# Down products of 768 tokens by a recursion of seven, with the sums of their weights made earlier in the program

## The chip, the core and the metric

One core of a Trainium2 chip runs the whole program in one launch. The engines of a core work side by side, each in the order of its own instruction list, and wait for each other by semaphores: TensorE (PE, matrix products; PEld is its loading of weights), VectorE (DVE), ScalarE (ACT), GpSimd (POOL) and SyncE (SP). SP and POOL issue the transfers between memory and the core's own buffers. The metric is the device time of one execution in microseconds (us); shown are the median, the lowest and the highest of three runs.

## The reference

One layer of a decoder for 1024 prompt tokens and 8 sample tokens that share the weights (model width 1024, width of the feed-forward part 2816):

```python
z = x @ w_in                                   # all branches and gates
a = rg_lru(conv4(...)) * gelu(...)             # recurrent branch
s = window attention, 16 query heads, 4 kv heads, window 128
c = attention over 256 memory tokens, 4 heads
merged = sum(gate[n] * (branch[n] @ w_branch[n]))
h = layer_norm(ALPHA * x + merged @ w_out)
gt, up = split(h @ w_gate_up)
h = layer_norm(ALPHA * h + (silu(gt) * up) @ w_down)
```

Besides h it returns the states of the branches; among them are the window caches of the 8 sample rows, moved on by one token (`o_swk`, `o_swv`). Everything is in fp32.

## The kernel before, in words

Activations lie transposed: 128 channels on the partitions, tokens along the free axis, 1032 of them. An fp32 product is made of three passes of a reduced type (fp32r): every operand is split into a high part, cast by ACT, and a low part, subtracted by DVE (`split`, L79 to L83), and PE runs high by high, low row by high weight, high row by low weight, into one accumulator. So 128 by 128 weights against n tokens are three matmuls of n columns. Weights arrive in pieces of up to 128 by 512 (`half_raw`, 6 buffers, issued by SP) and are split into pairs (`half_pair`, 5 buffers of high and 4 of low parts).

The program has these stages, in order: the projection, whose products run by a recursion of seven (2 by 2 blocks, seven products for eight); the branches a and c with the attentions; branch s (from about 1035 us); the output projection with its layer norm; two feed-forward units made directly (f = 0, 1); twenty units by the recursion of seven (f = 2 to 21, up to 1668.9 us); the down products (to 1925.3 us); and the end of the last layer norm.

A unit f makes one block of 128 of the 2816 feed-forward channels for all tokens. `unit_step` (L1198) issues the seven products i = 0 to 6 of a unit, each for two parts p of 258 columns. The end of a unit on DVE and ACT (L1236 to L1241) makes the gated value `ft`, which SP stores to a scratch row `scr_f` in memory. `fast_quarter` makes the sums of weights that i = 1, 2, 4 and 5 take, and splits them three steps ahead.

The down products (`down`, L1296) have 8 output blocks m, 22 rows f and three chunks of tokens (384, 384 and 264 wide). For each chunk and output the weights are read again and split again (`streamed`, L1274); a row of a chunk is read from `scr_f` by POOL (L1292) and split into a pair `gh`, `gl` (`rows`, L1287). Rows of the next chunk are fetched three with each output. The first chunk opens four accumulators on rows 0 to 11 at once, since the last units' rows come last. Result and residual are put together by DVE (L1339), a running sum is kept for the layer norm (L1341, L1343), and the norm of a chunk (`layer_norm`, L992) is dealt out in steps between the outputs of the next chunk (`norm_step`). The last chunk has its own norm (`last_layer_norm`, L1030), which follows the products closely.

What sets the order: a scheduler puts each engine's instructions in order from the program and from buffers; rooms (`gd`) of freed stages are laid over each other, so a load can start when the last reader of the stage that had the room is through. `issue_after(x)` holds instructions of x's own engine behind x.

Of the kernel before, what the change touches and what calls it, by code (L numbers as in the profile page):

```python
# [10 lines left out]
F32 = mybir.dt.float32  # L11
# [13 lines left out]
CH = ((0, 384), (384, 384), (768, 264))  # L25
# [4 lines left out]
DIRECT_AT = ((0, 258), (258, 258), (516, 252), (768, 264))  # L30
ROOMS = (*range(83, 67, -1), *range(36, 4, -1), *range(67, 36, -1), *range(4, -1, -1))
EARLY, EARLY_ROWS = ("mm", "s", "mm", "s"), 12
NORM_AT = (0, 1, 3, 4)
LATE = 4
# [24 lines left out]
class Builder:  # L59
# [223 lines left out]
    def fast_quarter(self, st, i):  # L283

        nc, ((a11, a12), (a21, a22)), u = self.nc, st["raw"], st["u"]
        if i in (1, 2, 4, 5):
            src = self.w1.tile([P, D // 2], F32, tag="sum", name=f"us{u}_{i}", bufs=self.sums)
# [693 lines left out]
    def col_mean(self, s, n, name):  # L981

        nc = self.nc
        hi = self.ph.tile([P, 384], F32R, tag="lh", name=f"{name}h", bufs=1)[:, :n]
        lo = self.ph.tile([P, 384], F32R, tag="ll", name=f"{name}l", bufs=1)[:, :n]
        self.split(hi, lo, s)
        ps = self.bank("o", f"{name}p")[:, :n]
# [4 lines left out]
    def layer_norm(self, c, r, s1, gcol, emit, name, late=False):  # L992
# [5 lines left out]
        mu = self.col_mean(s1, n, f"{name}mu{c}")  # L998
        s2 = ph.tile([P, 384], F32, tag="s2", name=f"{name}s2{c}", bufs=1)[:, :n]
        for m in range(KT):  # L1000
            nc.vector.tensor_sub(r[m], r[m], mu)
            sq = s2 if m == 0 else ph.tile([P, 384], F32, tag="sq", name=f"{name}sq{c}_{m}", bufs=2)[:, :n]
# [5 lines left out]
        var = self.col_mean(s2, n, f"{name}va{c}")  # L1008
        rs = ph.tile([P, 384], F32, tag="s2", name=f"{name}rs{c}", bufs=1)[:, :n]
# [20 lines left out]
    def last_layer_norm(self, n, r, product, gcol, emit):  # L1030
# [4 lines left out]
        tile_ = lambda tag, name, bufs, dt=F32: ph.tile([P, 384], dt, tag=tag, name=name, bufs=bufs)[:, :n]  # L1035
        s1, s2 = tile_("s1", "ls1", 1), tile_("s2", "ls2", 1)
        hi, lo = (ph.tile([P, n], F32R, tag=f"c0{e}", name=f"c0{e}", bufs=1) for e in "hl")
        e1, e2 = self.bank("t", "le1")[:, :n], self.bank("t", "le2")[:, :n]
# [13 lines left out]
        for m in range(KT):  # L1052
            ps = product(m, last=m < LATE)
            if m in NORM_AT:
                self.norm_step()
# [4 lines left out]
            if m == 1:  # L1060
                s = tile_("xres", "lc0", 3)
                nc.vector.tensor_add(s, r[0], r[1])
                self.split(hi, lo, s)
            elif m == LATE - 1:
                with self.tc.issue_after(self.last_mm):
                    c0 = self.bank("o", "c0")[:, :n]
# [11 lines left out]
        mu, rs = tile_("xres", "lmu", 3), tile_("gt", "lrs", 3)  # L1078
# [14 lines left out]
    def out_proj(self, merged):  # L1093
# [4 lines left out]
        for c, (t0, n) in enumerate(CH):  # L1098
            s1 = ph.tile([P, 384], F32, tag="s1", name=f"o1s{c}", bufs=1)[:, :n]
            rs = []  # L1100
            for m in range(KT):
                if c == 0:
                    w[m] = self.resident(io["wout"][m], KT, f"wo{m}", 0)
                ps = self.mm_res(w[m], merged, c, f"op{m}_{c}", tag=("mm", "s")[m % 2])
                if m in NORM_AT:
                    self.norm_step()
                xr = ph.tile([P, 384], F32, tag="xres", name=f"xres{m}_{c}", bufs=2)[:, :n]
# [17 lines left out]
    def direct_units(self):  # L1125
# [31 lines left out]
        for n, m, q in ((0, 0, 0), (3, 4, 0), (5, 4, 2)):  # L1157
            self.ht[n] = [[self.hl(m + k, (q + p) * QN, QN) for p in range(2)] for k in range(4)]
# [5 lines left out]
    def h_sums(self, i):  # L1164
# [12 lines left out]
        x = lambda kh, th, k: self.accs[4 * kh + k][:, th * HT:(th + 1) * HT]  # L1177
# [3 lines left out]
        for k in range(4):  # L1181
            if i == 1:
                t1 = wide("t1", k)
                nc.vector.tensor_sub(t1, x(0, 0, k), x(0, 1, k))
                pair(1, k, t1)
            elif i == 2:
                t3, t2 = wide("t3", k), wide("t2", k)
                nc.vector.tensor_sub(t3, x(1, 1, k), x(0, 1, k))
                nc.vector.tensor_add(t2, t3, x(0, 0, k))
# [3 lines left out]
            else:  # L1193
                t4 = wide("t4", k)
                nc.vector.tensor_sub(t4, self.t2[k], x(1, 0, k))
                pair(6, k, t4)

    def unit_step(self, st, i):  # L1198
# [3 lines left out]
        for p in range(2):  # L1202
# [32 lines left out]
            elif i == 5:  # L1235
                nc.vector.tensor_add(za[:, hi_], d, st["s", 2, p])  # L1236
# [345 lines left out]
```

## Time and profile before

| | |
|---|---|
| median of three runs (lowest to highest) | 1938.64 us (1937.28 to 1940.72) |
| the profiled execution, and its span | 1940.76 us, 1939.0 us |
| mean granted TensorE clock | 0.996 |
| PE busy | 1906.2 us (98%), 14356 matmuls |
| DVE busy | 1361.8 us (70%) |
| ACT busy | 1017.7 us (52%) |
| POOL busy | 154.0 us (8%) |
| the down stage's matmuls (L1283, L1284, L1285) | 528 each |
| read from memory, written | 214.64 MB, 66.85 MB |

The profile's rows name line, engine, operation and tiles (out<-in) and then the shape. Matmuls are pipelined: a row's duration overlaps the next one's, and what a matmul takes of PE's time is the distance from start to start. `dl` is an accumulator of the down stage, `wd_h` and `wd_l` are parts of a piece of its weights, `gh` and `gl` parts of a row, `fb` and `fd` accumulators of a unit, `bsH` and `bsL` the rows of branch s, `n2s` the running sum of squares in the second layer norm.

### The profile page before, as it was taken

Reading aid. Unit: us, or ns where it says so; the run is one execution under the profiler, and the core shown is the slowest. Engines: PE = TensorE matmul, PEld = TensorE weight load, DVE = VectorE, ACT = ScalarE, POOL = GpSimd, SP = SyncE. Lnnn points to the kernel's source line nnn. Section 1 sums busy time; section 2 is a strip of 40 time slices with the busy share of each in tenths; the row PEclk is TensorE's granted clock in tenths of the full one; section 3 lists DMA queues with packets and bytes.
Section 4 is the critical chain, followed back from the end, with each engine's and each line's share of the span. In section 5 each row is a group of like instructions: output and inputs, shape, how many; then the busy total and the mean of one; then the engine's idle time right before and its main releaser. Section 6 shows DMA issues by size and latency. Waiting matters only on the chain. (4 is left out here: it accounts for less than half of the span.)

```text
span 1939.0 us, 37975 instructions
## 1 busy us (share of the span) xinstructions
PE 1906.2 (98%) x14356; PEld 1882.2 (97%) x14356; DVE 1361.8 (70%) x2875; ACT 1017.7 (52%) x2198; POOL 154.0 (8%) x242
## 2 busy tenths in 40 slices
PE   8999999999999999999999999999999999999997
PEld 8999999999999999999999999999999999999997
DVE  8678887887777545379887558965665666747566
ACT  5465565456566545388875245643333433635444
POOL 1000000000011310022110000000000000402001
PEclk9999999999999999999999999999999999999999
DMA  7444545465323876567625241122222322846554
GB/s 232 145 161 147 170 169 186 131 204 181 126 91 127 285 239 202 158 177 201 173 77 183 88 150 42 39 88 88 88 82 82 99 74 80 278 131 187 159 155 139
DMA packets 169383, 281.92 MB, mean 145 GB/s; under 512 B 20864, under 2 KB 83408, under 8 KB 169168
## 3 DMA queue, kind: packets, MB, share of 16 engines
q1 hardware_dynamic: 163280, 262.62, 43.1%
q0 software_dynamic: 5920, 16.88, 2.6%
q8 instruction: 112, 1.84, 0.4%
q14 instruction: 71, 0.58, 0.1%
HBM read 214.64 MB, written 66.85 MB: 145 GB/s over the span
## 5 line engine op out<-in xcount | busy, mean ns | idle before, releaser
L1285 PE MATMUL dl<-gh,wd_l 128*128 128x384 f32 (+1 forms) x528 | 168.1, 318 | 3.1 <-DVE wd_l L82 3.1
L1283 PE MATMUL dl<-gh,wd_h 128*128 128x384 f32 (+1 forms) x528 | 167.7, 318 | 1.1 <-ACT gh L81 1.1
L1284 PE MATMUL dl<-gl,wd_h 128*128 128x384 f32 (+1 forms) x528 | 167.9, 318 | 0.0
L1285 PEld LDWEIGHTS dl<-gh,wd_l 128*128 128x128 f32 x528 | 99.7, 189 | 3.5 <-DVE wd_l L82 3.5
L1283 PEld LDWEIGHTS dl<-gh,wd_h 128*128 128x128 f32 x528 | 99.7, 189 | 1.3 <-ACT gh L81 1.3
L1284 PEld LDWEIGHTS dl<-gl,wd_h 128*128 128x128 f32 x528 | 99.8, 189 | 0.5 <-DVE gl L82 0.5
L1292 POOL DMA_DIRECT2D gl<-scr_f x66 | 35.6, 539 | 788.3 <-PE fb L1219 632.0
L81 ACT CAST u_1h<-us 128x512 fp32r<-128x512 f32 x48 | 29.8, 621 | 87.5 <-issue 43.5
L608 ACT ACTIVATE bp<-bp,bst 128x257 f32<-128x257 f32 (+1 forms) x128 | 62.3, 489 | 19.9 <-DVE bst L604 19.9
L81 ACT CAST u_2h<-us 128x512 fp32r<-128x512 f32 x48 | 29.7, 619 | 76.6 <-PE fb L1218 38.2
L289 DVE TENSOR_TENSOR us<-ur,ur 128x512 f32<-128x512 f32 x96 | 66.1, 688 | 4.3 <-DMA ur<-win 2.2
L289 DVE TENSOR_TENSOR us<-us,ur 128x512 f32<-128x512 f32 x96 | 66.2, 690 | 2.3
L82 DVE TENSOR_TENSOR u_6l<-ur,u_6h 128x512 fp32r<-128x512 f32 x48 | 33.9, 706 | 44.9 <-PE fb L1219 28.5
L117 PE MATMUL brs<-bsH,wbs_h 128*128 128x384 f32 (+1 forms) x192 | 61.0, 319 | 1.0 <-ACT bsH L81 1.0
L118 PE MATMUL brs<-bsL,wbs_h 128*128 128x384 f32 (+1 forms) x192 | 60.9, 318 | 0.3 <-DVE bsL L82 0.3
L119 PE MATMUL brs<-bsH,wbs_l 128*128 128x384 f32 (+1 forms) x192 | 60.9, 317 | 0.0
L82 DVE TENSOR_TENSOR u_4l<-us,u_4h 128x512 fp32r<-128x512 f32 x48 | 33.0, 688 | 39.7 <-PE fb L1219 27.4
L604 DVE CUSTOM_DVE_ANT_0 bp<-bs,mask,nsnk 128x256 f32<-128x256 f32 (+1 forms) x128 | 53.5, 459 | 5.2 <-PE bs L601 4.6
L82 DVE TENSOR_TENSOR u_5l<-us,u_5h 128x512 fp32r<-128x512 f32 x48 | 33.1, 690 | 30.0 <-PE fd L1219 14.5
L1237 ACT ACTIVATE ft<-za 128x516 f32<-128x516 f32 x40 | 25.5, 636 | 52.4 <-DVE za L1236 52.0
L81 ACT CAST u_5h<-us 128x512 fp32r<-128x512 f32 x48 | 29.9, 624 | 38.1 <-DVE us L289 24.9
L81 ACT CAST u_0h<-ur 128x512 fp32r<-128x512 f32 x48 | 29.8, 621 | 37.8 <-PE ub L306 20.1
(2022 smaller groups left out, 8123.4 us busy)
## 6 DMA issues: line engine op xcount, KB each, us to landing
ur<-win SPq DMA_DIRECT2D x112, 256.0 KB
ur<-wgu SPq DMA_DIRECT2D x80, 256.0 KB
scr_f<-ft SPq DMA_DIRECT2D x40, 258.0 KB
gl<-scr_f POOLq DMA_DIRECT2D x44, 192.0 KB, 4.1
dck<-cmk SPq DMA_DIRECT2D x32, 256.0 KB
dcv<-cmvT SPq DMA_DIRECT2D x32, 256.0 KB
st<-scr_q SPq DMA_DIRECT2D x32, 256.0 KB
scr_g<-za SPq DMA_DIRECT2D x10, 516.0 KB
```

The source lines that it names most:

```text
L81: ins = self.nc.scalar.copy(hi, src).ins
L82: self.nc.vector.tensor_sub(lo, src, hi.bitcast(F32))
L117: nc.tensor.matmul(ps, sh, mh, start=i == 0, stop=False)
L118: nc.tensor.matmul(ps, sh, ml, start=False, stop=False)
L119: self.last_mm = nc.tensor.matmul(ps, sl, mh, start=False, stop=closes and i == last).ins
L289: nc.vector.tensor_add(src, a, b)
L604: nc.vector.tensor_tensor_reduce(pg[g], s[:, u * 256:u * 256 + n], msk, 1.0, snk[:, g:g + 1], ALU.add, ALU.min, st[:, g:g + 1])
L608: nc.scalar.activation(x, x, AF.Exp, bias=st[:, g:g + 1], scale=-1.0, accum_out=st[:, 4 + g:5 + g])
L1283: nc.tensor.matmul(ps, sh, mh, start=k == 0, stop=False)
L1284: nc.tensor.matmul(ps, sh, ml, start=False, stop=False)
L1285: self.last_mm = nc.tensor.matmul(ps, sl, mh, start=False, stop=closes and k == NF - 1).ins
L1292: self.nc.gpsimd.dma_start(lo.bitcast(F32), self.scf[f][:, t0:t0 + n])
```

## The change

The 1032 tokens are seen as two halves of 516. Tokens 0 to 383 and 516 to 899 are the two sides of the recursion; the other 132 of each half are the rest (264). The 22 rows are two halves of 11, the 8 outputs are 4 pairs.

- The products of the 768 tokens: instead of 8 by 22 by 2 triples of matmuls, seven products (in the order 0, 3, 2, 1, 5, 4, 6), each 4 output pairs by 11 rows, 384 wide. Each of them takes either stored rows and stored weights or sums of such. A column (one pair's output) is 33 matmuls, with its weights in three pieces (4, 4 and 3 rows).
- The rest: 8 outputs by 22 rows by three matmuls of 264, in two halves of 11 rows; the first halves of m = 0 to 3 run ahead. The low parts of the weights of products 0, 3 and 6 are kept in rooms and used again here; for these pieces only the cast is made again.
- The sums of weights for products 1, 2, 4, 5: 16 jobs (`sum_turn`, `sum_load`, `sum_weights`), each 4 loads by POOL, 4 additions by DVE and 4 stores by POOL to a scratch. Eight are dealt out between the products of branch s, eight between the steps of the units f = 2 to 10.
- The sums of rows for products 1, 2, 4 and 6 (`row_load`, `row_sums`): ten jobs in the units f = 11 to 20, each 2 loads by POOL, 4 operations of DVE and 4 stores (from POOL, the last of these from SP). The eleventh (`last_sums`) runs after product 0 by SP.
- Rows: each product reads its 11 rows by POOL, in the course of the product before it.
- The end of the last unit (f = 21, i = 5 and 6: `unit_end`) is held back and issued behind the split of the first eight rows.
- The parts p of a unit are now the two halves of 516 tokens, and a store of `ft` is one contiguous piece for each. The chunks of the earlier stages are 384, 390 and 258 wide.
- The window caches are copied in 16 pieces, one in each unit from f = 4 on, instead of in two (f = 6 and 12).

Matmuls in the down stage: 1584 before (1056 of 384 and 528 of 264 columns), 1452 after (924 and 528). Transfers issued by POOL: 106 before (66 of them rows of the down stage), 323 after.

```diff
-CH = ((0, 384), (384, 384), (768, 264))
+CH = ((0, 384), (384, 390), (774, 258))
+DOWN_ORDER = (0, 3, 2, 1, 5, 4, 6)
+DOWN_PIECES = ((0, 4), (4, 4), (8, 3))
+SUM_PIECES = ((0, 3), (3, 3), (6, 3), (9, 2))
+KEPT = (0, 3, 6)
@@ branch s, out_proj, units
+                    self.sum_jobs = deque((j, e) for j in range(KT // 2) for e in range(len(SUM_PIECES)))
                     for _ in self.branch(2, "s"):
-                        pass
+                        self.sum_turn(6, 4)
...
+            if f < KD + 1:
+                self.sum_turn(8, 6)
+            if i == 3 and KD <= f < NF - 1:
+                early = self.row_load(f - KD)
+            if i == 1 and turn:
+                with self.tc.issue_after(self.last_mm):
+                    self.row_sums(*turn, self.nc.sync if f == NF - 1 else self.nc.gpsimd)
...
+    def sum_weights(self, j, o, n, raw):
+        nc, (a11, a12, a21, a22) = self.nc, raw
+        with self.tc.issue_after(self.last_mm):
+            nc.vector.tensor_add(a22, a21, a22)
+            nc.vector.tensor_add(a21, a11, a21)
+            nc.vector.tensor_add(a11, a22, a11)
+            nc.vector.tensor_add(a12, a11, a12)
+        for i, a in ((1, a22), (4, a21), (2, a11), (5, a12)):
+            nc.gpsimd.dma_start(self.scw[j][:, SUM_AT[i], o:o + n], a)
...
+    def down_begin(self):
+        self.norm, self.lows = None, {}
+        self.rooms()
+        first = partial(self.down_row, DOWN_ORDER[0])
+        self.first_rows = [first(k, "a") for k in range(8)]
+        self.first_weights = {(DOWN_ORDER[0], 0, e): self.down_weights(DOWN_ORDER[0], 0, e) for e in range(3)}
+        with self.tc.issue_after(self.row_cast):
+            self.first_weights.update({(DOWN_ORDER[0], 1, e): self.down_weights(DOWN_ORDER[0], 1, e) for e in range(3)})
+            for held in self.held:
+                held()
+        self.first_rows += [first(k, "a") for k in range(8, KD)]
...
+        for n, i in enumerate(DOWN_ORDER):
+            ahead = deque(range(KD))
+            for j in range(KT // 2):
...
+                for e, (k0, nk) in enumerate(DOWN_PIECES):
+                    wh, wl = self.weights_of(i, j, e)
+                    for k in range(k0, k0 + nk):
+                        w = slice((k - k0) * P, (k - k0 + 1) * P)
+                        xh, xl = act[k]
+                        mm(wh[:, w], xh, start=opens and k == 0, stop=False)
+                        mm(wh[:, w], xl, start=False, stop=False)
+                        self.last_mm = mm(wl[:, w], xh, start=False, stop=k == KD - 1).ins
+                    if ahead:
+                        k = ahead.popleft()
+                        if i == 6:
+                            last[k] = self.last_row(k)
+                        else:
+                            nxt[k] = self.down_row(DOWN_ORDER[n + 1], k, "ba"[n % 2])
+                    if i == 6 and (j, e) in ((1, 2), (2, 2)):
+                        self.norm_step()
+                evict(i, j, ps)
+            act = nxt
+            if i == 0:
+                self.last_sums()
+            if i == 4:
+                norm_of(1)
```

The change moves instructions at three places. The first is DVE's list where the units end and the down products begin. `ft`, `za`, `zb` are values of the last unit, `wd_.._l` and `wk` low parts of weights, `gl` low parts of rows (the first number behind a name is an output, a pair or a row's side). Before, the unit's end (L1236 to L1241) stood ahead of every row:

```order
L1238 SCALAR_TENSOR_TENSOR ft_1_21655<-ft_1_21655,za_1_21654 128x516
L1241 SCALAR_TENSOR_TENSOR ft_0_21639<-fb_0_21521,ft_0_21639 128x258
L1239 TENSOR_TENSOR ft_1_21655<-ft_1_21655,zb_1_21683 128x258
L1241 SCALAR_TENSOR_TENSOR ft_1_21655<-fb_1_21536,ft_1_21655 128x258
L82 TENSOR_TENSOR wd_1_00_l<-wd_1_0r__22005,wd_1_00_h 128x512
L82 TENSOR_TENSOR gl_0_21840<-gl_0_21840,gh_0_21839 128x384
L82 TENSOR_TENSOR gl_0_21845<-gl_0_21845,gh_0_21844 128x384
```

In the changed kernel (L92 is the same subtraction):

```order
L92 TENSOR_TENSOR gl_7_22293<-gl_7_22293,gh_7_22292 128x384
L92 TENSOR_TENSOR wk_1_0_22318<-wd_1_0r,wd_1_0h 128x512
L92 TENSOR_TENSOR wk_1_1_22324<-wd_1_1r,wd_1_1h 128x512
L92 TENSOR_TENSOR wk_1_2_22330<-wd_1_2r,wd_1_2h 128x384
L1257 SCALAR_TENSOR_TENSOR ft_0_22075<-ft_0_22075,za_0_22074 128x516
L1257 SCALAR_TENSOR_TENSOR ft_1_22091<-ft_1_22091,za_1_22090 128x516
L1258 TENSOR_TENSOR ft_0_22075<-ft_0_22075,zb_0_22105 128x258
L1258 TENSOR_TENSOR ft_1_22091<-ft_1_22091,zb_1_22119 128x258
L1260 SCALAR_TENSOR_TENSOR ft_0_22075<-fb_0_21949,ft_0_22075 128x258
L1260 SCALAR_TENSOR_TENSOR ft_1_22091<-fb_1_21964,ft_1_22091 128x258
L92 TENSOR_TENSOR gl_8_22346<-gl_8_22346,gh_8_22345 128x384
```

The unit's end now stands behind three pieces of weights, eight rows and three more pieces, and ahead of rows 8 to 10. On PE the first two columns (`dl_0`, `dl_1`) are taken in turns there, so that row 8 comes behind most of what rows 0 to 7 give:

```order
L1498 MATMUL dl_0_22366<-gh_7_22292,wk_0_1_22306 128x384
L1497 MATMUL dl_1_22416<-gl_0_22258,wd_1_0h 128x384
L1498 MATMUL dl_1_22416<-gh_0_22257,wk_1_0_22318 128x384
...
L1498 MATMUL dl_1_22416<-gh_3_22272,wk_1_0_22318 128x384
L1496 MATMUL dl_0_22366<-gh_8_22345,wd_0_2h 128x384
L1496 MATMUL dl_1_22416<-gh_4_22277,wd_1_1h 128x384
...
L1498 MATMUL dl_1_22416<-gh_7_22292,wk_1_1_22324 128x384
L1496 MATMUL dl_1_22416<-gh_8_22345,wd_1_2h 128x384
L1497 MATMUL dl_0_22366<-gl_8_22346,wd_0_2h 128x384
```

PE reaches the first low part of row 8 behind the 48 matmuls of rows 0 to 7 in both columns.

The second place is DVE's list at the start of branch s, where eight low parts of rows (`bsL`) were made in one run (L82, rows `bsL_0_14006` to `bsL_0_14027`). Now a sum of weights (`dw`, L1287 to L1290) stands between them:

```order
L92 TENSOR_TENSOR bsL_0_14027<-bsL_0_14027,bsH_0_14026 128x384
L1287 TENSOR_TENSOR dw_14163<-dw_14162,dw_14163 128x384
L92 TENSOR_TENSOR bsL_0_14030<-bsL_0_14030,bsH_0_14029 128x384
L92 TENSOR_TENSOR bsL_0_14033<-bsL_0_14033,bsH_0_14032 128x384
L92 TENSOR_TENSOR bsL_0_14036<-bsL_0_14036,bsH_0_14035 128x384
L1288 TENSOR_TENSOR dw_14162<-dw_14160,dw_14162 128x384
L92 TENSOR_TENSOR bsL_0_14039<-bsL_0_14039,bsH_0_14038 128x384
L92 TENSOR_TENSOR bsL_0_14042<-bsL_0_14042,bsH_0_14041 128x384
L1289 TENSOR_TENSOR dw_14160<-dw_14163,dw_14160 128x384
L1290 TENSOR_TENSOR dw_14161<-dw_14160,dw_14161 128x384
```

Two of the job's four additions stand ahead of the last low part of a row.

The third place is DVE's list in product 6, where the norm of the second side runs. `n2s` and `n2mu1p` belong to the norm, `wk_3_1` and `wk_3_2` to the last column of the product, `glc` are rows of the rest:

```order
L1011 TENSOR_TENSOR acc_15080<-acc_15080,n2mu1p 128x384
L1015 TENSOR_TENSOR n2s_24089<-n2s_24089,n2sq_6_24181 128x384
L1464 SCALAR_TENSOR_TENSOR acc_15078<-acc_15078,dl_2_22466 128x384
L1015 TENSOR_TENSOR n2s_24089<-n2s_24089,n2sq_7_24185 128x384
L1474 TENSOR_TENSOR o2s_22364<-o2s_22364,acc_15078 128x384
L92 TENSOR_TENSOR wk_3_1_24216<-wd_3_1r,wd_3_1h 128x512
L92 TENSOR_TENSOR wk_3_2_24239<-wd_3_2r,wd_3_2h 128x384
L92 TENSOR_TENSOR glc_24254<-glc_24254,ghc_24253 128x264
```

Fifteen operations of the norm stand ahead of the piece `wk_3_1`. Before, the same kind of work stood ahead of a piece of the last chunk (L1005 ahead of `wd_l`).

More of the change, by code (lines that the diff above doesn't have):

```diff
@@ L1270, in units @@
             if i == 6:
+                if KD <= f < NF - 1:
+                    k = f - KD
+                    turn = (k, *early, *(st[f]["t", p][:, :NA] for p in range(2)),
+                            *(self.scratch(f"rs{k}{x}", NA) for x in range(2)))
                 del st[f]
         yield
[L1274 to L1285 removed]
@@ new lines, in down, with emit_to, emit @@
+        at = (0, HT)
+        r = [[a[:, o:o + NA] for a in self.accs] for o in at]
+        act = self.first_rows
+        banks = {}
+        s1 = [ph.tile([P, CW], F32, tag=f"s1{x}", name=f"o2s{x}", bufs=1)[:, :NA] for x in range(2)]
+        done = [[], []]
+        def emit_to(dst):
+            def emit(m, v, scale=1.0):
+                nc.scalar.activation(v, v, AF.Identity, bias=self.vec[:, V_B2 + m:V_B2 + m + 1], scale=scale)
+                nc.sync.dma_start(dst(m), v)
+            return emit
@@ new lines, in down, with half @@
+        for f in range(KD, NF):
+            last[f] = self.last_row(f)
+        open_ = {}
+        def half(m, kh, ps, closes):
+            for e, (k0, nk) in enumerate(DOWN_PIECES):
+                wh, wl = self.last_weights(m, kh, e)
+                for k in range(k0, k0 + nk):
+                    w = slice((k - k0) * P, (k - k0 + 1) * P)
+                    xh, xl = last[kh * KD + k]
+                    nc.tensor.matmul(ps, wh[:, w], xh, start=kh + k == 0, stop=False)
+                    nc.tensor.matmul(ps, wh[:, w], xl, start=False, stop=False)
+                    self.last_mm = nc.tensor.matmul(ps, wl[:, w], xh, start=False,
+                                                    stop=closes and kh == 1 and k == KD - 1).ins
@@ new lines, in down, with product @@
+        for m in range(EARLY):
+            open_[m] = self.bank(("mm", "s")[m % 2], f"dc{m}")[:, :2 * NC]
+            half(m, 0, open_[m], False)
+            self.norm_step()
+            if m == EARLY - 2:
+                norm_of(0)
+        def product(m, closes=True):
+            if m not in open_:
+                open_[m] = self.bank(("mm", "s")[m % 2], f"dc{m}")[:, :2 * NC]
+                half(m, 0, open_[m], False)
+            half(m, 1, open_[m], closes)
+            return open_[m]
@@ L1346, in build @@
+        tail = lambda a: a.rearrange("p (q n) -> p q n", q=2)
+        rows = [tail(a)[:, :, NA:] for a in self.accs]
+        self.last_layer_norm(2 * NC, rows, product, V_G2, emit_to(lambda m: tail(io["o_y"][:, m, :])[:, :, NA:]), tail)
     def build(self):
@@ L1416, in build @@
                 hy.close()
+                ea.close()
                 with pool("w2") as self.w2:
-                    next(units)
-                late.close()
-                rows.close()
-                with pool("ph6") as self.ph, pool("gd", "right") as self.gd:
+                    with pool("xs", "right") as self.xs:
+                        next(units)
+                    late.close()
+                    rows.close()
+                    rooms = ExitStack()
+                    self.gd = rooms.enter_context(pool("gd", "right"))
+                    self.down_begin()
+                with pool("ph6") as self.ph:
                     self.down()
+                rooms.close()
 class Finish:
```

293 lines of the change are left out of this document (190 added, 103 removed).

## The prediction

> **What bounds the kernel now.** I read the page's busy times first, then its costliest groups, then PE's waits, then PE's timeline where the waits lie.
>
> ```profile
> PE 1906.2 (98%) x14356; PEld 1882.2 (97%) x14356; DVE 1361.8 (70%) x2875; ACT 1017.7 (52%) x2198; POOL 154.0 (8%) x242
> L1285 PE MATMUL dl<-gh,wd_l 128*128 128x384 f32 (+1 forms) x528 | 168.1, 318 | 3.1 <-DVE wd_l L82 3.1
> L1283 PE MATMUL dl<-gh,wd_h 128*128 128x384 f32 (+1 forms) x528 | 167.7, 318 | 1.1 <-ACT gh L81 1.1
> L1284 PE MATMUL dl<-gl,wd_h 128*128 128x384 f32 (+1 forms) x528 | 167.9, 318 | 0.0
> ```
>
> PE is busy for 98% of the span, so a matmul less is time less, as long as nothing else takes its place. The last column of the groups (idle before, and who ended it) gives the down stage 4.2 us of waits in some 255 us. The mean of 318 ns is no price: rows of a pipelined PE overlap. The price is the distance of starts, which a stretch without waits shows:
>
> ```profile
> L1284 PE MATMUL dl<-gl,wd_h x135: 334/334/338, 1779.8 to 1849.9; 128*128 128x384 f32 x135
> ```
>
> 135 triples begin within 70.1 us, so one of them takes 70.1 / 134 = 0.523 us and one matmul of 384 columns 0.1744 us. What the stage loses stands in PE's timeline (start, duration, [idle before]):
>
> ```profile
> 1668.78 0.28 PE L1219 MATMUL fb<-h_3h,u_6l 128*128 128x258 f32 x1
> 1670.11 0.62 PE L1283 MATMUL dl<-gh,wd_h 128*128 128x384 f32 x2 [1.05 <-ACT gh L81]
> ...
> 1869.76 0.28 PE L1285 MATMUL dl<-gh,wd_l 128*128 128x264 f32 x1
> ...
> 1870.72 0.28 PE L1284 MATMUL dl<-gl,wd_h 128*128 128x264 f32 x1
> 1873.17 0.39 PE L1285 MATMUL dl<-gh,wd_l 128*128 128x264 f32 x1 [2.17 <-DVE wd_l L82]
> ...
> 1874.12 0.40 PE L1283 MATMUL dl<-gh,wd_h 128*128 128x264 f32 x1
> ...
> 1877.39 0.36 PE L1283 MATMUL dl<-gh,wd_h 128*128 128x264 f32 x1
> ...
> 1899.57 0.28 PE L1284 MATMUL dl<-gl,wd_h 128*128 128x264 f32 x1
> 1900.74 0.39 PE L1285 MATMUL dl<-gh,wd_l 128*128 128x264 f32 x1 [0.89 <-DVE wd_l L82]
> ```
>
> A 264-wide matmul takes 0.12 us (eight from 1869.76 to 1870.72; the 258-wide ones alike). So the handover from the units costs 1670.11 - 1668.78 - 0.12 = 1.2 us, the wait for a low part of weights at 1870.72 costs 2.3, the one at 1899.57 costs 1.05. Behind the 2.3 us gap come 15 matmuls from 1874.12 to 1877.39 at 0.218 instead of 0.12: 1.5 us more. Together 6.05 us.
>
> **What is removed.** 1584 matmuls become 1452; the 528 of 264 columns remain and 1056 of 384 become 924. 132 x 0.1744 = **23.0 us**. That holds if 384-wide matmuls keep their distance when DVE and the transfers beside them have more to do.
>
> The Trainium skill ("TensorE: Matmul & The Clock Gate", section "Wait — 56ns, not 53.3ns?") has N / 2.4 GHz + 2.5 ns from start to start: 162.5 ns at 384, which would make the term 21.5 us; the row's 174.4 ns decides.
>
> **What is added beside PE in the down stage.** Prices of DVE, from neighbouring starts:
>
> ```profile
> 1200.31 0.55 DVE L1005 TENSOR_TENSOR n1s<-n1s,n1sq 128x384 f32<-128x384 f32 x1
> 1200.78 0.55 DVE L1001 TENSOR_TENSOR acc<-acc,n1mu1p 128x384 f32<-128x384 f32 x1
> ...
> 1873.03 0.43 DVE L82 TENSOR_TENSOR c0l<-lc,c0h 128x264 fp32r<-128x264 f32 x1
> 1873.37 0.69 DVE L82 TENSOR_TENSOR wd_l<-wd_4r__24196,wd_h 128x512 fp32r<-128x512 f32 x1
> 1873.97 0.68 DVE L82 TENSOR_TENSOR wd_l<-wd_8r__24214,wd_h 128x512 fp32r<-128x512 f32 x1
> ...
> 1208.11 2.55 DVE L1013 RECIPROCAL n1rs<-n1rs 128x384 f32<-128x384 f32 x1 [0.54 <-ACT n1rs L1010]
> ```
>
> 0.47 us for 384 columns, 0.34 for 264, 0.60 for 512. A product needs of DVE 8 pieces of 512 and 4 of 384 (6.7 us), 11 rows (5.2), 4 results and up to 4 running sums (3.8): 15.7 us. PE needs 132 x 0.1744 = 23.0 us for it, so DVE is at two thirds. The profile has stretches of 23 us of both kinds (PE, PEld, DVE, ACT, POOL busy, clock, DMA share, GB/s):
>
> ```profile
> 1668.00:1691.00 23.00, 21.95 (x127) 21.23 (x127) 22.26 (x46) 20.44 (x46) 11.28 (x21) 1.00 0.91 314
> 1714.00:1737.00 23.00, 23.00 (x134) 23.00 (x133) 9.76 (x17) 7.04 (x12) 0.00 (x0) 1.00 0.47 133
> 1760.00:1783.00 23.00, 23.00 (x135) 23.00 (x134) 21.27 (x47) 16.20 (x37) 4.59 (x9) 1.00 0.64 196
> ```
>
> In the third, DVE has 21.27 of 23 us, rows and weights arrive at 196 GB/s, and PE does not stop. A product reads 44 blocks of weights of 64 KB and 11 rows of 192 KB, 5 MB or 219 GB/s: between the third and the first stretch. I cost the steady product at nothing; its cover is PE itself, as long as DVE's in-order list doesn't hold the next piece behind a result that PE has not finished.
>
> POOL issues 99 rows instead of 66.
>
> ```profile
> L1292 POOL DMA_DIRECT2D gl<-scr_f x42: 536/536/605, 1650.9 to 1687.7; - x42
> DMA to landing us min/median/max: 3.5/4.1/6.1
> ```
>
> Eleven issues are 6 us of 23, and a room of the next product's rows is free a whole product ahead, so 6.1 us to landing are hidden.
>
> **The handover.** DVE's list now has three pieces (1.7 us), eight rows (3.7), three pieces (1.7), the unit's end, and rows 8 to 10 (1.4). The unit's end costs two of L1238 at 0.61 and four of L1239 and L1241 at 0.35, 2.6 us:
>
> ```profile
> 1667.80 0.69 DVE L1238 SCALAR_TENSOR_TENSOR ft<-ft,za 128x516 f32<-128x516 f32 x1
> 1668.41 0.42 DVE L1241 SCALAR_TENSOR_TENSOR ft<-fb,ft 128x258 f32<-128x258 f32 x1
> 1668.74 0.42 DVE L1239 TENSOR_TENSOR ft<-ft,zb 128x258 f32<-128x258 f32 x1
> ```
>
> DVE is free of i = 5 about 2.1 us before the units' last matmul ends (24 matmuls of 0.12 follow i = 5, less two additions). From that end, the first row is split at +0.1, row 7 at +3.4, the pieces of the second column at +5.0, row 8 at +8.1. PE has 48 matmuls on rows 0 to 7, until +8.4, then 18 more and four of the next columns, until about +12.2. The third column's first low part comes behind the results of the first two columns, at about +13. So some 0.9 us are lost, where 1.2 were; bounds 0 and the 2.6 us by which the held end could come ahead of what PE needs.
>
> **The norms at the end.** In product 6 fifteen operations of the norm (7.0 us) stand ahead of `wk_3_1`; PE has the column before (33 matmuls, 5.7 us), 14 of the last and 15 of the rest beside them, 10.0 us: no loss. Later the variance's low part behind five rows (0.6) and the pieces behind the reciprocal and eight scalings (2.5 + 8 x 0.5 us, against a column of 33 x 0.12 and 6 fillers; 1.3) cost about 1.9. With the handover 2.8 us are lost in place of 6.05: **3.2 saved**; bounds 6 (none lost) and 0.
>
> **The sums in branch s.** Its start is tight:
>
> ```profile
> 1035.00:1055.00 20.00, 19.00 (x113) 18.69 (x114) 17.39 (x39) 12.35 (x30) 0.00 (x0) 1.00 0.71 236
> 1036.00 4.00 DVE L82 TENSOR_TENSOR bsL<-bsL,bsH 128x384 fp32r<-128x384 f32 x8
> ```
>
> Eight low parts take DVE 4.0 us with PE right behind (8 x 0.523 = 4.2). Two additions between them are 0.94 us with 0.2 of slack: 0.7 lost. If the four loads land late, DVE stands at the first addition with five low parts behind it: two transfers' 4.1 us, about 4. The other seven jobs cost 1.6 us each in a stretch where DVE has some room. I take **1.5**; bounds 0 and 4.
>
> **The sums in the units.**
>
> ```profile
> 1340.00:1500.00 160.00, 159.36 (x1331) 159.15 (x1330) 95.04 (x179) 58.81 (x118) 0.00 (x0) 1.00 0.28 90
> ```
>
> DVE has 59% there; 4 operations of 0.47 in each unit (168 matmuls; 160 / 1331 x 168 = 20.2 us) make it 68%, hidden behind PE unless a low part of weights comes late. Ten transfers of POOL a unit add to a DMA share of 0.28. I take **1.0**; bounds 0 and 2. The copies in pieces and the chunks of 390 and 258 columns move the same bytes and columns: nothing, either way.
>
> **The boundaries of products.** Six times the rows, banks and sources change. No row shows such a change; the nearest are the chunk changes of before, which cost nothing at the second chunk (third stretch above) and 2.3 + 1.5 in the last. I take **2.0** in all, nearer the former; bounds 0 and 6 x 1.2.
>
> **Sum.** Against the profiled execution, 1940.76 (span 1939.0): -23.0 - 3.2 + 1.5 + 1.0 + 2.0 = -21.7, so 1919.1. It lies 2.1 above the median of the runs; for the median, 1938.64 - 21.7 = **1917**. Best ends: -23.0 - 6 = 1909.6. Worst ends: -23.0 + 4 + 2 + 7.2 = 1928.8.
>
> **Rivals.**
>
> A, every boundary stalls briefly: at each of six boundaries and into the rest, DVE waits for a column's result and then still has a 512-wide piece and a row ahead of what PE needs. Seven gaps of 1.2 to 2.3 us in place of the 2.0: 1923 to 1931. For it: three of the four losses before have this form. Against it: the changed list has the next column's pieces ahead of most results.
>
> B, nothing is lost: all bounds at their good ends, 1909 to 1912. For it, the third stretch; against it, the last norm's reciprocal, which no order hides.
>
> C, slower: the clock. One gap of 2.3 us was followed by 1.5 us of half-speed work, those of 1.05 and 1.2 by none, so the point lies between. If DVE's list gives all seven places a gap of 2.3 us or more, each costs 2.3 + 1.5 = 3.8, together 26.6, and nothing is saved at the old places: 1938.64 - 23.0 + 26.6 + 1.5 + 1.0 = 1945 (1941, about no change, with six of them). Against it: DVE has 7 us to spare in each product.
>
> The Trainium skill (same page, "What's actually happening") sets the half clock after an idle window of some 3.4 us that runs freely; the row shows it after 2.3 us, so gaps shorter than that page's window already count here.
>
> D, matmuls are removed but the rest run slower: with 0.2 instead of 0.1744 us for 924 matmuls all of it is lost (23.7 us) and the time is within 4 us of 1938. The first stretch, with 314 GB/s and DVE busy for 22.26 of 23 us, speaks against it: 127 matmuls in 21.95 us of work are 0.173 each.
>
> **Chances.** The forecast with its own range (1912 to 1923) 0.66; A 0.16; B 0.07; C 0.07; D 0.04. About 0.2% (3.9 us) is what a measurement of this kernel tells from no change. Faster by more than that: forecast, A, B, 0.89; within: D, 0.04; slower: C, 0.07. The range for 8 in 10 goes from 1911, into B, to 1930, through most of A.
>
> **What would show it.** A distance of 0.174 us between 384-wide matmuls in the new products; PE's waits under `wk`, `wd_l` and `gl` of at most 2 us each, the largest at the handover's third column and behind the last reciprocal; a granted clock of 1.00 in all seven products; branch s longer by 0 to 4 us, a unit still at 20.2. Waits of 2.3 us or more followed by distances near 0.22 or 0.33, or units that take longer by over 0.2 us each, would make the prediction wrong.

## The result: 1958.5 us, slower, and the profile after

| | before | changed |
|---|---|---|
| median of four runs (lowest to highest) | 1939.06 us (1937.28 to 1940.72) | 1958.51 us (1955.67 to 1962.40) |
| profiled execution, its span | 1940.76, 1939.0 us | 1959.74, 1957.9 us |
| mean granted TensorE clock | 0.996 | 0.990 |

The ratio is 1.0102 (95% interval 1.0081 to 1.0123). Forecast were 1917 us, 1911 to 1930: the time is outside the range, and the kernel became slower where it was to become faster.

Where the 19 us of span lie is read from PE's timeline, from the first matmul of each stage to the first of the next (us; the units end 0.12 us after their last matmul begins, the products where the sums `le` of the last norm begin):

| stage | before | changed | difference |
|---|---|---|---|
| up to branch s | 1035.7 | 1036.1 | +0.4 |
| branch s | 90.7 | 109.3 | **+18.6** |
| output projection, direct units | 138.4 | 139.3 | +0.9 |
| twenty units | 404.1 | 422.7 | **+18.6** |
| handover and down products | 256.2 | 235.6 | **-20.6** |
| after the last product | 13.9 | 15.0 | +1.1 |

So the recursion gives about what it should, and two stages whose products were not touched lose nearly twice that. These are single executions: in a later run (the row sums alone held) branch s, with the same instructions, took 106.1 us instead of 109.3. The page of the changed kernel, its busy times and the groups with the new idle times (busy, mean | idle before, releaser):

```profile
PE 1894.7 (97%) x14224; PEld 1867.4 (95%) x14224; DVE 1399.3 (71%) x2980; ACT 1023.5 (52%) x2219; POOL 273.7 (14%) x459
...
L127 PE MATMUL brs<-bsH,wbs_h 128*128 128x384 f32 (+2 forms) x192 | 62.5, 328 | 13.4 <-DVE gts L690 12.3
...
L1287 DVE TENSOR_TENSOR dw<-dw,dw 128x384 f32<-128x384 f32 (+1 forms) x16 | 8.4, 525 | 63.2 <-DMA dw<-wdn 54.9
```

The third row is the case: the first addition of a weight sum costs DVE 8.4 us of work for all 16 jobs, and 63.2 us of standing, 54.9 of them with its loads (`dw` from `wdn`) named as what ended it. The windows of the two stages, before (branch s, then 100 us of units):

```profile
1036.00:1126.00 90.00, 89.67 (x574) 89.39 (x573) 56.16 (x118) 31.19 (x73) 0.00 (x0) 1.00 0.40 129
1265.00:1365.00 100.00, 100.00 (x837) 100.00 (x836) 62.88 (x118) 38.74 (x78) 0.00 (x0) 1.00 0.26 82
```

and of the changed kernel:

```profile
1036.00:1145.00 109.00, 95.04 (x573) 92.26 (x574) 65.93 (x143) 29.34 (x66) 32.63 (x60) 0.97 0.60 199
1285.00:1385.00 100.00, 85.66 (x683) 84.43 (x681) 65.97 (x129) 31.79 (x66) 34.71 (x64) 0.95 0.56 179
```

The same 573 matmuls of branch s lie in 109 us instead of 90; PE is idle for 14.0 us of them, and its busy time has grown by 5.4 us; the mean granted clock fell to 0.97 (some 2.2 of the 5.4 us are half-speed matmuls behind the longest gap, shown next). DVE, at 66 of 109 us, is far from full. How one of these waits looks, in DVE's timeline of the changed kernel (start, duration, [idle before]):

```profile
1099.43 0.56 DVE L92 TENSOR_TENSOR H_4l<-M,H_4h 128x384 fp32r<-128x384 f32 x1 [0.58 <-ACT H_4h L91]
1106.44 0.56 DVE L1287 TENSOR_TENSOR dw<-dw,dw 128x384 f32<-128x384 f32 x1 [6.45 <-DMA dw<-wdn]
1106.92 0.55 DVE L690 SCALAR_TENSOR_TENSOR gts<-gts,brs 128x390 f32<-128x390 f32 x1
```

in POOL's:

```profile
1099.12 0.54 POOL L1280 DMA_DIRECT2D dw<-wdn  x1
1103.03 1.22 POOL L1280 DMA_DIRECT2D dw<-wdn  x2 [3.37 <-DMA scr_w<-dw]
```

and in PE's:

```profile
1102.52 0.34 PE L129 MATMUL brs<-bsH,wbs_l 128*128 128x384 f32 x1
1107.53 0.69 PE L127 MATMUL brs<-bsH,wbs_h 128*128 128x390 f32 x1 [4.67 <-DVE gts L690]
```

The additions of this job stand in DVE's list ahead of `gts` (L690), which empties an accumulator. The job's last two loads could go out only at 1103.0, when the stores of the job before had landed and its rooms were free. DVE stands for 6.45 us, and PE, out of accumulators, for 4.67. The next 15 matmuls begin 0.325 us apart instead of 0.178.

In the units the jobs are dealt out one in eight steps by the program, some 23 us. In DVE's list all eight stand in f = 2 to 5, one behind the other, and the distances of unit starts are 20.77, 22.45, 28.74, 21.87 and 27.37 us for f = 2 to 6 and 20.1 for every unit after that. The last job shows the same picture as in branch s: its first addition stands ahead of the operation that makes `ft` of f = 5, and f = 6 waits for that.

```profile
1380.54 0.43 DVE L1287 TENSOR_TENSOR dw<-dw,dw 128x256 f32<-128x256 f32 x1 [5.01 <-DMA dw<-wdn]
1385.10 0.42 DVE L1260 SCALAR_TENSOR_TENSOR ft<-fb,ft 128x258 f32<-128x258 f32 x1
1385.57 0.58 PE L1229 MATMUL fb<-H_0h,u_0h 128*128 128x258 f32 x1 [5.49 <-DVE ft L1260]
```

The five units lose 20.7 us against 20.11 each; the stage shows 18.6, since two other units became 0.92 shorter (the window caches, below).

### The profile page after: what moved, and what is told of

The parts are those of the page before. It is cut to its first block, busy times and chain, and to the rows that moved or that the text cites. A ratio compares the mean times of both kernels' runs of the same rounds, so it can differ in the third digit from the quotient of the medians.

```text
span 1957.9 us, 38236 instructions
## 1 busy us (share of the span) xinstructions
PE 1894.7 (97%) x14224; PEld 1867.4 (95%) x14224; DVE 1399.3 (71%) x2980; ACT 1023.5 (52%) x2219; POOL 273.7 (14%) x459
## 4 chain that ended last, share of the span: by engine, by line
PE 64%; issue 16%; DMA 10%; DVE 5%; ACT 3%; POOL 2%; SPq 0%; POOLq 0%; DVEq 0%; ACTq 0%
PE ub L315 5%; PE ub L316 5%; PE ub L317 5%; PE fb L1229 3%; PE fb L1230 3%; PE fb L1231 3%; DMA scr_w<-dw 3%; PE ud L316 2%; PE ud L315 2%; PE ud L317 2%; DMA dw<-wdn 2%; PE fd L1230 2%; PE fd L1231 2%; PE fd L1229 2%; PE brc L128 1%
## 5 line engine op out<-in xcount | busy, mean ns | idle before, releaser
L127 PE MATMUL brs<-bsH,wbs_h 128*128 128x384 f32 (+2 forms) x192 | 62.5, 328 | 13.4 <-DVE gts L690 12.3
L128 PE MATMUL brs<-bsL,wbs_h 128*128 128x384 f32 (+2 forms) x192 | 62.3, 325 | 1.5 <-DVE bsL L92 1.5
L1280 POOL DMA_DIRECT2D dw<-wdn x64 | 34.8, 543 | 203.0 <-DVE h_3l L92 152.3
L129 PE MATMUL brs<-bsH,wbs_l 128*128 128x384 f32 (+2 forms) x192 | 62.1, 324 | 0.0
L806 POOL TENSOR_SCALAR tr<-th 128x1032 f32<-128x1032 f32 x8 | 11.0, 1369 | 311.5 <-DVE sq L805 103.9
L1287 DVE TENSOR_TENSOR dw<-dw,dw 128x384 f32<-128x384 f32 (+1 forms) x16 | 8.4, 525 | 63.2 <-DMA dw<-wdn 54.9
L92 DVE TENSOR_TENSOR u_5l<-us,u_5h 128x512 fp32r<-128x512 f32 x48 | 33.1, 690 | 28.5 <-PE fd L1231 13.8
L92 DVE TENSOR_TENSOR gl<-gl,gh 128x384 fp32r<-128x384 f32 x77 | 39.9, 553 | 16.9 <-ACT gh L91 16.7
L127 PEld LDWEIGHTS brs<-bsH,wbs_h 128*128 128x128 f32 x192 | 36.9, 193 | 15.6 <-DVE gts L690 12.8
L92 DVE TENSOR_TENSOR u_6l<-ur,u_6h 128x512 fp32r<-128x512 f32 x48 | 33.0, 687 | 25.8 <-PE ub L317 16.3
L625 POOL TENSOR_SCALAR bp<-bp,bst 128x256 f32<-128x256 f32 (+1 forms) x32 | 32.8, 1023 | 130.0 <-DVE bst L619 129.9
L91 ACT CAST gh<-gl 128x384 fp32r<-128x384 f32 x77 | 36.7, 511 | 24.1 <-DMA gl<-scr_s 17.2
L1498 PE MATMUL dl<-gh,wk 128*128 128x384 f32 x132 | 44.4, 337 | 3.5 <-DVE wk L92 3.5
```

The lines of the kernel that those rows point to most:

```text
L91: ins = self.nc.scalar.copy(hi, src).ins
L92: self.nc.vector.tensor_sub(lo, src, hi.bitcast(F32))
L127: nc.tensor.matmul(ps, sh, mh, start=i == 0, stop=False)
L128: nc.tensor.matmul(ps, sh, ml, start=False, stop=False)
```

## The experiments

The theory (H): the additions are held behind the last matmul, which orders PE's list and nothing of DVE's. In DVE's list they stand as early as the order reckons their loads, ahead of work for which PE waits; the loads come later than reckoned, DVE's list stands, PE starves. Against it stood T, the transfers themselves (128 more through POOL, the DMA share from 0.40 to 0.60 in branch s), and R, the four rooms that a job has to wait for.

### The additions left out

```diff
-        with self.tc.issue_after(self.last_mm):
-            nc.vector.tensor_add(a22, a21, a22)
-            nc.vector.tensor_add(a21, a11, a21)
-            nc.vector.tensor_add(a11, a22, a11)
-            nc.vector.tensor_add(a12, a11, a12)
```

> The changed kernel without the four additions of each weight sum (L1287 to L1290); the 64 loads and 64 stores stay, so the stored sums are the raw pieces and the down products of 1, 2, 4, 5 come out of wrong weights. Theory H (DVE's in-order list waits for the sums' loads, 37 us in branch s and 26 us in the units, and PE starves behind it): branch s goes from 109.3 back to about 91 us, the units from 422.6 to 404 to 407, the whole to 1920 to 1925. Rival T (the added transfers themselves delay weights or matmuls): nothing comes back, 1953 to 1960.

Measured: 1943.24 us, ratio to before 1.0016 (1.0007 to 1.0026). Branch s came back to 93.6 us, the units only to 418.7, the whole neither to H's time nor to T's. What was left in the units is one gap; PE's waits from 1270 to 1400 us in this run:

```profile
PE fb L1229 <- DVE zb L1246: 13.0, 1, 13.0
```

and DVE's there:

```profile
DVE rs L1298 <- DMA rx<-scr_f: 19.7, 1, 19.7
```

`rs` is the first operation of the first row sum. It needs two loads of an old row (`rx`) and nothing else, so it moved to f = 4, eight units ahead of its place, and waited for loads that stand in POOL's list behind all 16 jobs. The same mechanism, in a place that the first statement of H had left out.

### The additions held on DVE

```diff
-        with self.tc.issue_after(self.last_mm):
+        with self.tc.issue_after(self.last_dve):
             nc.vector.tensor_add(a22, a21, a22)
...
```

`last_dve` is the last low part that DVE was given; `split` notes it.

> The changed kernel with the four additions held behind the last low part that DVE was given ahead of them in the program (a DVE instruction) instead of the last matmul. In DVE's list the 16 jobs then stand where the program has them: four in branch s, four in the output projection, eight in f = 2 to 11. Theory H: the loads have landed by then; branch s about 92 to 94, units 404 to 407, up to 1.9 us for each of the four jobs in the output projection, whole 1922 to 1932. Rival T: the same transfers over twice the time, 1940 to 1955.

Measured: 1923.62 us (1921.57 to 1925.13), ratio 0.9915 (0.9896 to 0.9934): faster than before, by an edit that removes no transfer and no operation. Branch s takes 92.2 us, the units 402.1, every unit 20.1 or 20.2; the output projection, which now has four jobs, 139.5 (138.4 before). DVE's longest waits in branch s (1036 to 1130 us) are again waits for PE:

```profile
DVE gts L690 <- PE brs L129: 21.9, 18, 2.0
DVE bsL L92 <- ACT bsH L91: 1.6, 2, 1.1
```

Of the 16 jobs, 15 now begin their additions without any standing of DVE. One, in the output projection, still waits for its loads, and there PE has no wait:

```profile
1143.98 0.56 DVE L1287 TENSOR_TENSOR dw<-dw,dw 128x384 f32<-128x384 f32 x1 [5.13 <-DMA dw<-wdn]
```

The program deals four of the first eight jobs out in branch s and four in the output projection (the description of the change puts all eight in branch s). Unheld, all eight stood in branch s; held, four do. So this run also thins out the transfers there (DMA share 0.55, from 0.60), and does not by itself rule T out for that stage.

### The additions on POOL, and the row sums held

> The changed kernel with the four additions of each weight sum on POOL instead of DVE. Theory H: only POOL's list waits, DVE's none, 1920 to 1926 with no DVE wait on these loads. Rival T: transfers unchanged, 1953 to 1960. Should POOL's additions slow DVE beside them, branch s stays some us longer than 91.

With `nc.gpsimd.tensor_add` in place of the four additions, and no hold on them: 1962.49 us, ratio 1.0117 (1.0099 to 1.0134), far from H's time and a little above T's. Yet the units (438.0 us) lose nearly all of it in one place again (f = 5 takes 53.89 us), at the first row sum, whose loads stand behind POOL's longer list; DVE's waits in the units:

```profile
DVE rs L1302 <- DMA rx<-scr_f: 53.2, 10, 36.9
```

The two runs that hold the row sums also (`self.last_mm` replaced by `self.last_dve` ahead of `row_sums`) decide it:

> The run without the additions of the weight sums (their stored values again the raw pieces), with one thing more: the row sums are held behind the last low part that DVE was given ahead of them. Theory H, mended: what was left of the loss without the additions was the first operation of the first row sum, which DVE's list had at f = 4 and which waited 19.7 us for its loads behind all 16 jobs in POOL's list; held, that wait is gone, the units are back at 402 to 404 us from 418.7, the whole at 1924 to 1929. Rival T (the transfers themselves cost what was left): no change, 1940 to 1946.

Measured 1925.00 us, ratio 0.9918 (0.9900 to 0.9936); units 402.1 us from 418.7. H as mended. This run also decides against T in branch s: its window

```profile
1037.00:1131.00 94.00, 92.83 (x574) 89.80 (x575) 56.65 (x117) 32.17 (x74) 25.96 (x49) 1.00 0.65 224
```

has a DMA share of 0.65 and 224 GB/s, more than the change's 0.60 and 199, and the stage takes 94.2 us, not 109.3.

> The additions of the weight sums on POOL, and the row sums held as well. Theory H: the 36.9 us wait of DVE for the first row sum's loads goes, 1962.5 - 34 = 1926 to 1931. Rival T: POOL's additions and transfers cost it all the same, 1950 to 1963.

Measured 1932.48 us, ratio 0.9959 (0.9945 to 0.9974), units 404.7 us from 438.0. A little above what was expected: branch s stays at 97.8, 3.6 us longer than with no additions at all. POOL's additions slow DVE beside them: for about as many instructions (116 against 117) DVE is busy for 69.65 us of branch s, against 56.65 in the window above. A 512-wide low part, 0.68 us elsewhere, took 1.89 us beside such additions:

```profile
1036.00:1134.00 98.00, 93.94 (x574) 91.03 (x575) 69.65 (x116) 30.58 (x70) 56.14 (x83) 0.98 0.66 224
1288.63 1.89 DVE L92 TENSOR_TENSOR u_1l<-us,u_1h 128x512 fp32r<-128x512 f32 x1
1288.93 1.03 POOL L1288 TENSOR_TENSOR dw<-dw,dw 128x384 f32<-128x384 f32 x1
```

T keeps a small rest: with all additions gone and the row sums held, branch s takes 94.2 us, 3.5 more than before. These lie in small pieces that were not followed; PE's one longer wait, 2.0 us for ACT's cast of a row, ends with the stage's first matmul and so lies ahead of it.

### More rooms

```diff
-        return self.xs.tile([P, NA], F32, tag="xs", name=name, bufs=4)[:, :n]
+        return self.xs.tile([P, NA], F32, tag="xs", name=name, bufs=self.xn)[:, :n]
```

`xn` is 6 in branch s and 5 in the units.

> The changed kernel with 6 rooms (branch s) and 5 (units) instead of 4 for the pieces of the sums, additions as in the change. Rival R (the job's loads are late because they wait for the stores of the job before to free the four rooms): the loads of two of four pieces go out earlier in branch s, one in the units, and the waits shrink by a third or more, 1938 to 1950. Theory H (the order puts the additions at the time it reckons for the loads, whatever the rooms): the jobs only move closer together, 1950 to 1962.

Measured 1950.24 us, ratio 1.0055 (1.0040 to 1.0071), at the border of the two. By stages it is clear: branch s, with two rooms more, 99.8 us from 109.3; the units, with one more, 422.7, as with four. So R is a part of H: the rooms make the loads late, and the place in DVE's list makes it matter. Held in place, four rooms are enough.

### The row sums alone held

> The change itself with the row sums alone held, the additions of the weight sums as in the change. Theory H: in the change the first row sum waited 3.5 us only, since the weight sums had already kept POOL's list short; branch s 109, units 419 to 423, whole 1954 to 1959. Rival (the row sums are the larger part of the loss in the units): units under 412, whole under 1948.

Measured 1956.52 us, ratio 1.0102 (1.0082 to 1.0121), branch s 106.1, units 423.3 us. The total does not differ from the change's by more than the intervals. In the change itself the weight sums were the loss, not the row sums.

### The end of the down stage

Three runs on the waits that were forecast at 1.9 us behind product 6. PE's timeline of the changed kernel there, the rows with a wait:

```profile
1871.04 0.44 PE L1498 MATMUL dl<-gh,wk 128*128 128x384 f32 x1 [2.18 <-DVE wk L92]
1882.02 0.39 PE L1526 MATMUL dc<-ghc,wl_2l 128*128 128x264 f32 x1 [1.76 <-DVE wl_2l L92]
...
1891.77 0.39 PE L1526 MATMUL dc<-ghc,wl_1l 128*128 128x264 f32 x1 [1.63 <-DVE wl_1l L92]
```

The first reading put the 2.18 us to the norm's fifteen operations ahead of `wk_3_1`. The first of the three runs moves the norm's second step:

```diff
-                    if i == 6 and (j, e) in ((1, 2), (2, 2)):
+                    if i == 6 and (j, e) in ((1, 2), (3, 2)):
```

> Both kinds of sums held behind a DVE instruction, and the second step of the norm in product 6 given behind the last column's last piece instead of the column before's. Theory N (in product 6 PE waits 2.3 us for the piece wk_3_1 because fifteen operations of the norm stand ahead of it in DVE's list): that wait falls under 0.5 us, the rest of the end unchanged or a little later, 1919 to 1922. Rival: the norm is only pushed on into the 264-wide part, whose waits grow by as much, 1923 to 1925.

Measured 1921.58 us, ratio 0.9904 (0.9887 to 0.9922), and a down stage of 238.4 us, 2.3 longer than with the additions alone held (236.1). PE's waits at the end:

```profile
PE n2va1p L999 <- DVE n2va1l L92: 4.1, 1, 4.1
PE n2va1p L998 <- ACT n2va1h L91: 2.2, 1, 2.2
PE dl L1498 <- DVE wk L92: 0.3, 1, 0.3
```

The wait for `wk` is gone, as said, and the variance's matmuls wait 6.3 us instead, with 2.9 us of slower matmuls behind it: what the rival had, though the total lies in N's range. The total's gain against the held run is within the intervals. What the low part `n2va1l` stood behind is not the norm alone; rows of the 264-wide part come one by one ahead of it, with 3.4 us of DVE's standing at four of them, among these

```profile
1839.34 0.43 DVE L92 TENSOR_TENSOR glc<-glc,ghc 128x264 fp32r<-128x264 f32 x1 [0.76 <-ACT ghc L91]
1839.69 0.55 DVE L92 TENSOR_TENSOR n2va1l<-n2s,n2va1h 128x384 fp32r<-128x384 f32 x1
```

Then the variance was given a column later:

```diff
             half(m, 0, open_[m], False)
-            self.norm_step()
-            if m == EARLY - 2:
+            if m:
+                self.norm_step()
+            if m == EARLY - 1:
                 norm_of(0)
...
-LAST_AT = (0, 2, 3, 4)
+LAST_AT = (0, 1, 2, 3, 4)
```

> As the run with both kinds of sums held and the norm's second step behind the last column, but the norm's variance and scaling one column later in the 264-wide part, and the steps of the other side's norm after them. Theory N2 (the norm's 1 + 15 + 9 operations of DVE have to go where PE does not need a low part next; the columns m = 0 and 2 need none): the waits for the variance, 6.3 us, and the half-speed matmuls behind them, some 3 us, go, the down stage falls from 238.4 to 229 to 232 us, the whole to 1912 to 1917. Rival: the norms push the last layer norm, and the end grows by as much: 1919 to 1923.

Measured 1924.56 us, ratio 0.9929 (0.9916 to 0.9941), down stage 237.3 us. N2 falls, and the total lies above the rival's range too. PE now waits as long for a low part of weights:

```profile
PE dc L1526 <- DVE wl_0l L92: 6.3, 1, 6.3
```

In DVE's timeline ahead of it stand not norms but rows of the 264-wide part, one by one as they land:

```profile
1838.81 0.43 DVE L92 TENSOR_TENSOR glc<-glc,ghc 128x264 fp32r<-128x264 f32 x1 [0.31 <-ACT ghc L91]
1839.86 0.43 DVE L92 TENSOR_TENSOR glc<-glc,ghc 128x264 fp32r<-128x264 f32 x1 [0.61 <-ACT ghc L91]
1840.91 0.43 DVE L92 TENSOR_TENSOR glc<-glc,ghc 128x264 fp32r<-128x264 f32 x1 [0.62 <-ACT ghc L91]
1841.26 0.68 DVE L92 TENSOR_TENSOR wl_0l<-wl_0r,wl_0h 128x512 fp32r<-128x512 f32 x1
```

So rows 11 to 21, needed two columns and more later, were held behind the weights of m = 1 on DVE and ACT:

```diff
-        for f in range(KD, NF):
-            last[f] = self.last_row(f)
...
+            if m == 1:
+                with self.tc.issue_after(self.last_dve), self.tc.issue_after(self.last_act):
+                    for f in range(KD, NF):
+                        last[f] = self.last_row(f)
```

> As the run before (sums held, norm and variance later), and rows 11 to 21 of the 264-wide part, whose low parts stood in DVE's list ahead of the weights of m = 1 and waited one by one for their loads (1.1 us apart), now held behind those weights. Theory L (DVE's list waits for loads of rows that PE needs 16 us later): the 6.3 us wait for wl_0l goes and the half-speed matmuls behind it, the down stage falls from 237.3 to 228 to 231 us, the whole to 1913 to 1918. Rival (PE then waits for these rows themselves, or the norms, as late): 1921 to 1925.

Measured 1921.75 us (1917.29 to 1925.79), ratio 0.9910 (0.9892 to 0.9927). The time is in the rival's range. The down stage falls to 234.9 us, the wait for `wl_0l` is gone, and 3.6 us of wait for ACT's cast of the next weights stand in its place; in ACT's list that cast stands behind the casts of the last of these rows, which wait up to 1.5 us each for their loads. So the mechanism is the one of the sums, an in-order list with a load ahead of work that is due, and the hold moved it from DVE's list to ACT's. What it is worth here is not shown: the total's gain is not clear of the intervals. How much of the end can be had is open; by their intervals the four held runs with all additions differ by less than they are uncertain.

### The window caches in two pieces again

The units of the held run took 402.1 us, 2.0 less than before the change, where the prediction had nothing. Before, f = 8 and f = 14 had taken 21.03 us and all others 20.11; two units ahead of each, the whole cache was copied.

```diff
-            if i == 2 and f > 3 and caches:
-                name, cache, b = caches.popleft()
+            if (f, i) in ((6, 2), (12, 2)):
+                name, cache = ("o_swk", "cwk") if f == 6 else ("o_swv", "cwv")
                 with self.tc.issue_after(self.last_load):
-                    self.nc.sync.dma_start(io[name][b, 0:P - 1, :], io[cache][b, 1:P, :])
+                    self.nc.sync.dma_start(io[name][:, 0:P - 1, :], io[cache][:, 1:P, :])
```

> The changed kernel with the additions held, and the window caches copied in two pieces (f = 6 and 12) as before, instead of 16. If the two units before that took 21.03 us instead of 20.11 (f = 8 and 14) owed it to the copies, two units show it again and the units' stage goes from 402.1 back to about 403.9 us; if not (it came with the interleaved stores of ft, which stay as changed), all units remain at 20.1 and the stage at 402.1.

One execution, 1925.61 us; units 404.9 us, f = 8 at 21.01 and f = 14 at 22.06, the others at 20.1 or 20.2. PE's waits in the units:

```profile
PE fb L1231 <- DVE u_0l L92: 1.3, 2, 0.6
PE fd L1231 <- DVE u_1l L92: 0.4, 1, 0.4
```

The first row holds one wait of 0.63 us in f = 8 and one in f = 14; before the change PE waited 0.64 us for `u_0l` in the same two units. So the copies in two pieces cost the two units their time, and copying in pieces is worth some 2 us (2.8 by this one execution, whose f = 14 is a further 1.0 longer than before; that was not followed).

## Why the prediction was wrong, step by step

- **What bounds the kernel, and what is removed** (23.0 us): right. 384-wide matmuls keep their distance in the new products: in the changed kernel 827 of them lie in the 144 us from 1722 to 1866, 0.174 apart.

```profile
1722.00:1866.00 144.00, 143.74 (x827) 142.88 (x826) 99.68 (x193) 72.27 (x147) 37.60 (x66) 1.00 0.70 219
```

- **The steady product at nothing, the boundaries at 2.0 us**: the cover held. Between 1722 and 1866 us, through most of the seven products and all the boundaries between them, PE waits 0.3 us in all; the boundaries cost nothing. Rivals A and C, which put their losses there, did not occur.
- **The handover** (0.9 us, the third column's first low part): right in place, 1.04 us of wait. The start itself, which the sum did not price apart, is seamless: the first `dl` follows the last `fb` at 0.12 us.

```profile
1707.23 0.28 PE L1231 MATMUL fb<-h_3h,u_6l 128*128 128x258 f32 x1
1707.35 0.34 PE L1496 MATMUL dl<-gh,wd_0h 128*128 128x384 f32 x1
...
1720.71 0.45 PE L1498 MATMUL dl<-gh,wk 128*128 128x384 f32 x1 [1.04 <-DVE wk L92]
```

- **The norms at the end** (1.9 us, and `wk_3_1` at none): mis-sized. The three waits shown above come to 5.6 us; the matmuls behind them run at full speed. For `wk_3_1` the step counted 7.0 us of the norm; with one result and two running sums among them DVE works 8.4 us without a pause, from 1861.91 to 1870.31, ahead of that piece, and PE stood from 1868.86. At 1882.02 it is rows that arrive late (1.07 and 0.72 us of DVE's standing ahead of `wl_2l`), at 1891.77 it is the scalings, as the step had it (1.6 us where it had 1.3). So the down stage gained 20.6 us where the sum had 23.0 + 3.2 - 2.0 = 24.2.
- **The sums in branch s** (1.5 us, bounds 0 and 4): wrong, +18.6. This term and the next are the step that failed. The step saw the mechanism, DVE standing at an addition with other work behind it, and priced it for the first job alone, which cost nothing that shows: its loads had landed, and PE has no wait among the low parts between which its additions stand (one of 1.2 us ten us later, at 1051.06, was not followed). The other seven were priced as work, 1.6 us each "where DVE has some room". But jobs 3 to 8 cost PE 12.3 us of idling in six waits, beside the slow clock:

```profile
PE brs L127 <- DVE gts L690: 12.3, 6, 4.7
```

  What was not reckoned is the job's own round: four loads, landing, additions, four stores, landing, and only then the rooms are free. The jobs' additions begin 10 to 18 us apart (1037.79, 1055.40, 1071.89, 1082.49, 1092.58, 1106.44, 1122.57, 1135.43), as fast as the rooms turn, and DVE's list keeps that pace.
- **The sums in the units** (1.0 us, bounds 0 and 2): wrong, +20.7 in f = 2 to 6. The step took the program's places, one job in a unit with its loads six steps ahead. The order of the changed kernel, which could have been read, has all eight in f = 2 to 5. DVE's share of 68% was right and beside the point: a list that stands is not busy.
- **The copies at nothing**: off by 2 us, in the change's favour.
- **The rivals.** Slower had a chance of 0.07, by a clock that halves at the boundaries of products. The half clock was there, behind the longest gaps (4.67 us in branch s, 5.71 and 5.49 in the units), as the consequence of waits in stages that the rivals did not look at. Gaps of 2.88 and 2.28 us in branch s and of 2.18 in product 6 were followed by full speed, so rival C's price for every gap of 2.3 us or more, taken from the one such gap before the change, does not hold. No rival had DVE's list standing for loads in stages whose PE work is unchanged.

With the sums held in place the rest of the prediction holds within its range: the stages of the held kernel differ from before by +1.7 (up to branch s), +1.5 (branch s), +1.1 (output projection), -2.0 (units), -20.1 (down) and +1.0 (end), together -16.8 us where the prediction had -21.7, and its 1923.62 us lie between 1911 and 1930. That the term of 1.5 for branch s meets the held run's +1.5 is luck: it was reckoned for eight jobs there, and four stand there.

## What to carry to other kernels

Work added to an in-order engine "where it has room" is priced by when its inputs arrive, not by its busy time: look up its place in that engine's list, and what stands right behind it. A hold must name an instruction of the engine whose list it is to order; a hold on another engine leaves the scheduler free to move the instruction ahead to where it believes the load has landed. Where a side job turns a few rooms around (load, use, store, load), work out the round first; if the list lets it run at that pace, nearly every round ends in a wait (14 of the 16 jobs here).

## What the hardware showed beyond that

After the 4.67 us gap in branch s, 15 matmuls of 390 columns began 0.325 us apart instead of 0.178, about 2.2 us more; the gap cost half as much again as it lasted. Not so after the 2.18 us gap in product 6; the windows behind the two (the granted clock is the number behind POOL's):

```profile
1107.00:1112.00 5.00, 4.47 (x14) 4.48 (x15) 5.00 (x11) 1.44 (x3) 2.27 (x5) 0.50 0.51 174
1871.00:1876.00 5.00, 4.96 (x32) 4.96 (x33) 3.07 (x8) 2.05 (x6) 2.13 (x3) 1.00 0.75 231
```

Before the change a gap of the same 2.17 us was followed by a clock of 0.52. So the length of a gap alone does not settle, in these traces, whether half speed follows; what else does was not tested.

The Trainium skill ("TensorE: Matmul & The Clock Gate", section "Wait — 56ns, not 53.3ns?") gives N / 1.2 GHz for the half clock, an estimate of 325 ns at 390 columns, which the trace has exactly. The rule for full speed in the same section of the Trainium skill makes an estimate of 162.5 ns at 384 columns; the trace has 174.

A POOL load of a `dw` piece landed 4.2 us after its issue and a store 2.9 us (medians of the profile's page). With eight issues of 0.54 us and four additions of 0.47 us that makes an estimate of some 13 us for a round of one job, for 1.9 us of DVE's time; the distances above are 10 to 18 us.

```profile
dw<-wdn POOLq DMA_DIRECT2D x48, 192.0 KB, 4.2
scr_w<-dw POOLq DMA_DIRECT2D x48, 192.0 KB, 2.9
```
